# State products of a chunked scan as three split-operand matmuls, with the inputs' lower parts on GpSimd

## The chip, the cores and the metric

The kernel runs on one core of a Trainium2 chip. Its engines work side by side, each through its own queue of instructions in a fixed order, and wait for one another by semaphores: TensorE (PE in the profile; its weight loads are PEld), VectorE (DVE), ScalarE (ACT), GpSimd (POOL) and SyncE (SP), which issues most transfers. The metric is the device time of one execution in microseconds (us). Shorter is better.

## The reference

The program is one inference step of a small trunk: one Mamba-2 (SSD) layer, one pooling layer and a final norm, for a prompt of 1024 tokens and for 8 sampled sequences of 8 tokens each. The change lies in the SSD layer's scan. Cut to what it touches:

```python
T = min(CHUNK, L)            # 128 tokens
acum = jnp.cumsum(dt * A.reshape(G, R), axis=2)
CB = jnp.einsum('bctgn,bcsgn->bctsg', C, B)
xdt = x * dt[..., None]
y_intra = jnp.einsum('bctsgr,bcsgrp->bctgrp', CB[..., None] * decay, xdt)
decay_end = jnp.exp(acum[:, :, -1:] - acum)
chunk_states = jnp.einsum('bctgn,bctgr,bctgrp->bcgrpn', B, decay_end, xdt)
chunk_decay = jnp.exp(acum[:, :, -1])
def step(h, inp):
    s, d = inp
    return d[..., None, None] * h + s, h
h_final, h_prev = lax.scan(step, h0, (chunk_states, chunk_decay))
y_inter = jnp.einsum('bctgn,bctgr,bcgrpn->bctgrp', C, jnp.exp(acum), h_prev)
```

There are 32 heads of 64 channels in 8 groups of 4; a group shares B and C, with a state of 128 numbers per channel. So for each group and each of the prompt's 8 chunks a chunk state is one product of B (128 tokens by 128 states, transposed) with the decayed inputs (128 tokens by 256 channels).

## The kernel before

`ssd_layer` runs eight calls of `scan_group`, one per group. Each is woven with other work by `weave`, which takes steps of two generators in turn: groups 0 to 6 with `proj_group`, the input projection and convolution of the next group, group 7 with the first units of the output projection. Beneath this a scheduler of the tile framework places every engine's instructions in an order of its own, by its planned costs, and puts in the waits; so a step of the code doesn't stay where the source has it.

Within a group, `front(c)` prepares chunk c and `back(c)` finishes it; the loop calls `front(c + 1)` ahead of `back(c)`. Chunk 8 is the sample chunk. The names are:

- `front`: `pt` (tag tr, two buffers in PSUM) holds CB and the transposes of the two x tiles and of B. M is the decay times CB: four Relus and an Exp on ScalarE (L526, L527), cb and the product on VectorE (L529, L530). `xd` (L532, VectorE, two buffers) holds the inputs twice, scaled by dt and by dt times the decay to the chunk's end. `Bt` (L536, ScalarE) is B's transpose, copied out of PSUM; in the sample chunk it is split into `Bt` and its lower part `Bl` (L539, L540). `ea` (L513, L545) is C times the decay from the chunk's start, and `cd` (L544) the chunk's decay.
- `back`: four heads' y products, M by xd and ea by h (L560, L564), two at a time on halves of TensorE's columns (column-tiled); their evacuation on VectorE (L550); the state product `S` (L567); `hd`, the old state times `cd`, on GpSimd (L573); and the new state `h`, hd plus S, on VectorE (L574; a plain copy, L570, in chunk 0).
- `back_sample` and `state_sample`: the sample's states, with masked copies of the split inputs (`st`, L612 and L613; `xm` and `xs`, L616 to L618) against `Bt` and `Bl` (L625, L626).
- `proj_group`: matmuls of 364 or 360 columns in three parts (`mm3`, L178 to L180: upper weights by upper activations, upper by lower, lower by upper), their evacuation (L386, L388), the convolution `conv_tile` (ScalarE L342, three taps on VectorE L344, tanh L347, L348, L350), and the split of the next weights into an upper part (ScalarE L135) and a lower part (VectorE L136). The gate's squares are summed on TensorE (`ms`, L664).

In this trace a matmul of float32 operands shows as two passes (two records) and one of operands of the type F32R as one. The kernel splits a float32 operand into a copy in F32R (the upper part) and the difference, in F32R as well (the lower part), and multiplies two such operands in three products: upper by upper, upper by lower, lower by upper.

Of the kernel before, what the change touches and what calls it, by code (L numbers as in the profile page):

```python
# [7 lines left out]
F32 = mybir.dt.float32  # L8
F32R = mybir.dt.float32r
AF = mybir.ActivationFunctionType  # L10
ALU = mybir.AluOpType
# [3 lines left out]
P = 128  # L15
# [78 lines left out]
class Build:  # L94
# [379 lines left out]
    def scan_group(self, g, T):  # L474
        nc, tk, gp, pp = self.nc, self.tk, self.gs, self.pp
        B, C, xs, zs = T[0], T[1], T[2:4], []
# [17 lines left out]
        def load_ac(c):  # L494
            if c < 8:
                j, cc = c // 2, c % 2
                t = gp.tile([P, 4, 128], F32, tag="acb", bufs=2, name=self.name("acb"))
                nc.sync.dma_start(t, self.acd[32 * j + 4 * g:32 * j + 4 * g + 4, 128 * cc:128 * cc + 128].unsqueeze(0).to_broadcast([P, 4, 128]))
            else:
                t = gp.tile([P, 4, 128], F32, tag="acb", bufs=2, name=self.name("acb"))[:, :, :64]  # L500
                nc.sync.dma_start(t, self.acd[96 + 4 * g:100 + 4 * g, 256:320].unsqueeze(0).to_broadcast([P, 4, 64]))
            acbs[c] = t

        def front(c):

            j, cc, L = (c // 2, c % 2, 128) if c < 8 else (0, 2, 64)
            col = 32 * j + 4 * g
            t0 = 128 * c
            tok = slice(t0, t0 + L)
            acb = acbs.pop(c)  # L510
            load_ac(c + 1) if c < 8 else None
            ea = gp.tile([P, 4, 128], F32, tag="ea", bufs=2, name=self.name("ea"))
            nc.scalar.activation(ea[:, :, :L], acb, AF.Exp)  # L513
            pt = pp.tile([P, 512], F32, tag="tr", bufs=2, name=self.name("tr"))
            nc.tensor.matmul(pt[:L, 384:384 + L], B[:, tok], C[:, tok], start=True, stop=True)
            for i, t in enumerate((xs[0], xs[1], B)):
                o = pt[:, 128 * i:128 * i + 128]
                if c < 8:
                    nc.tensor.transpose(o, t[:, tok], self.ident)
                else:  # L520
                    self.dup(o, t[:, tok])

            M = gp.tile([P, 4, 128], F32, tag="M", bufs=2, name=self.name("M"))
            mask = self.kc[:L, K_MASK:K_MASK + 128] if c < 8 else self.kc[:64, K_SMASK:K_SMASK + 64]
            for r in range(4):
                nc.scalar.activation(M[:L, r, :L], acb[:L, r, :], AF.Relu, bias=tk["ac", cc][:L, col + r:col + r + 1], scale=-1.0)  # L526
            nc.scalar.activation(M[:L, :, :L], M[:L, :, :L], AF.Exp, scale=-1.0)  # L527
            cb = gp.tile([P, 128], F32, tag="cb", bufs=1, name=self.name("cb"))
            nc.vector.tensor_tensor(out=cb[:L, :L], in0=pt[:L, 384:384 + L], in1=mask, op=ALU.mult)  # L529
            nc.vector.tensor_tensor(out=M[:L, :, :L], in0=M[:L, :, :L], in1=cb[:L, :L].unsqueeze(1).to_broadcast([L, 4, L]), op=ALU.mult)  # L530
            xd = gp.tile([P, 2, 4, 64], F32, tag="xd", bufs=2, name=self.name("xd"))
            nc.vector.tensor_tensor(out=xd, in0=pt[:, 0:256].rearrange("p (r q) -> p r q", r=4).unsqueeze(1).to_broadcast([P, 2, 4, 64]),  # L532
                                    in1=tk["x", cc][:, :, col:col + 4].unsqueeze(3).to_broadcast([P, 2, 4, 64]), op=ALU.mult)
            if c < 8:
                Bt = gp.tile([P, 128], F32, tag="Bt", bufs=2, name=self.name("Bt"))
                nc.scalar.activation(Bt, pt[:, 256:384], AF.Copy)  # L536
            else:
                Bt = tuple(gp.tile([P, 128], F32R, tag=s, bufs=2, name=self.name(s)) for s in ("Bt", "Bl"))
                nc.scalar.activation(Bt[0], pt[:, 256:384], AF.Copy)  # L539
                nc.vector.tensor_tensor(out=Bt[1], in0=pt[:, 256:384], in1=Bt[0].bitcast(F32), op=ALU.subtract)  # L540
            cd = None
            if 0 < c < 8:
                cd = gp.tile([P, 4], F32, tag="cd", bufs=2, name=self.name("cd"))
                nc.scalar.activation(cd, acb[:, :, 127], AF.Exp)  # L544
                nc.vector.tensor_tensor(out=ea, in0=C[:, tok].unsqueeze(1).to_broadcast([P, 4, 128]), in1=ea, op=ALU.mult)  # L545
            return tok, M, xd[:, 0], xd[:, 1], Bt, cd, ea

        def evac_y(py, q, tok, L):
            y = xs[q]
            nc.vector.scalar_tensor_tensor(out=y[:, tok], in0=y[:, tok], scalar=self.vec[:, V_D + 2 * g + q:V_D + 2 * g + q + 1], in1=py[:, :L],  # L550
                                           op0=ALU.mult, op1=ALU.add)

        def back(c, F):
            nonlocal h
            tok, M, xdt, xde, Bt, cd, ct = F
            for q in range(2):
                py = pp.tile([P, 512], F32, tag="y", bufs=2, name=self.name("y"))
                for rr in range(2):
                    r, o = 2 * q + rr, slice(64 * rr, 64 * rr + 64)
                    nc.tensor.matmul(py[o, :128], xdt[:, r, :], M[:, r, :], start=True, stop=(h is None))  # L560
                if h is not None:
                    for rr in range(2):
                        r, o = 2 * q + rr, slice(64 * rr, 64 * rr + 64)
                        nc.tensor.matmul(py[o, :128], h[:, r, :], ct[:, r, :], start=False, stop=True)  # L564
                evac_y(py, q, tok, 128)
            S = pp.tile([P, 512], F32, tag="S", bufs=1, name=self.name("S"))
            nc.tensor.matmul(S[:, :256], Bt, xde.rearrange("p r q -> p (r q)"), start=True, stop=True)  # L567
            hn = gp.tile([P, 4, 64], F32, tag="h", bufs=3, name=self.name("h"))
            if h is None:
                nc.vector.tensor_copy(hn.rearrange("p r q -> p (r q)"), S[:, :256])  # L570
            else:
                hd = gp.tile([P, 4, 64], F32, tag="hd", bufs=1, name=self.name("hd"))
                nc.gpsimd.tensor_tensor(out=hd, in0=h, in1=cd.unsqueeze(2).to_broadcast([P, 4, 64]), op=ALU.mult)  # L573
                nc.vector.tensor_tensor(out=hn, in0=hd, in1=S[:, :256].rearrange("p (r q) -> p r q", r=4), op=ALU.add)  # L574
            h = hn
# [19 lines left out]
        def back_sample(F, zsc):  # L595
            tok, M, xdt, xde, Bt, _, ea = F
            for q in range(2):
                py = pp.tile([P, 512], F32, tag="y", bufs=2, name=self.name("y"))
                for rr in range(2):
                    r, o = 2 * q + rr, slice(64 * rr, 64 * rr + 64)  # L600
                    nc.tensor.matmul(py[o, :64], xdt[:64, r, :], M[:64, r, :64], start=True, stop=False)
                for rr in range(2):
                    r, o = 2 * q + rr, slice(64 * rr, 64 * rr + 64)
                    nc.tensor.matmul(py[o, :64], zsc[:, r, :], self.kc[:, K_SEL64:K_SEL64 + 64], start=False, stop=True)
                evac_y(py, q, tok, 64)
            for i in range(2):
                nc.gpsimd.tensor_tensor(out=h0[i], in0=h0[i],
                                        in1=ea[:, :, 32 * i + 7:32 * i + 32:8].rearrange("p r b -> p b r").unsqueeze(3).to_broadcast([P, 4, 4, 64]), op=ALU.mult)

            xv = xde.rearrange("p r q -> p (r q)")  # L610
            st = gp.tile([P, 256], F32R, tag="xl", bufs=1, name=self.name("st"))
            nc.scalar.activation(st, xv, AF.Copy)  # L612
            nc.vector.tensor_tensor(out=st[64:], in0=xv[64:], in1=st[64:].bitcast(F32), op=ALU.subtract)  # L613
            xms = []
            for b2 in range(4):
                xm = gp.tile([P, 2, 256], F32R, tag=("xm", "xs")[b2 % 2], bufs=2, name=self.name("xs"))  # L616
                for i in range(2):
                    nc.scalar.activation(xm[:, i], st.bitcast(F32), AF.Copy, scale=self.kc[:, K_SEQ + 2 * b2 + i:K_SEQ + 2 * b2 + i + 1])  # L618
                xms.append(xm.rearrange("p b n -> p (b n)"))
            return xms, Bt  # L620
# [10 lines left out]

        load_ac(0)
        F = front(0)
        yield
        for c in range(8):
# [1133 lines left out]
```

## Time and profile before

| | |
|---|---|
| time, median of 3 runs | 1660.68 us (1660.06 to 1662.37) |
| the profiled execution | 1660.51 us, of which the span is 1658.7 us |
| granted TensorE clock, mean | 0.994 |
| busy, share of the span | PE 98%, PEld 93%, DVE 79%, ACT 50%, POOL 29% |
| the scan | from about 265 to 880 us |
| DMA | 251 MB in all, mean 151 GB/s |

The profile gives one execution. Its page has the busy time of each engine over the span, the same in 40 equal slices with the clock that TensorE was granted, the chain of work that ended last, and the costliest groups of instructions by source line. Views of the trace give single instructions in a stretch of time (start and duration in us, then engine, line, operation, output and inputs, shape and count; in brackets the idle time before it and what ended it), the waits of an engine by what they were for, and sums by stretch. The durations of matmuls overlap, since they are pipelined: what a matmul costs is the distance between the ends of two of them.

### The profile page before, as it was taken

The page shows a single profiled execution, that of the slowest core. Times are in us where ns is not written, and L with a number is a line of the kernel's source. Part 1 is how long each engine was busy: PE and PEld are TensorE (multiplying, and loading weights), DVE is VectorE, ACT ScalarE, POOL GpSimd, SP SyncE. Part 2 cuts the span into 40 slices and gives each one's busy share as a digit, 9 for nine tenths or more (in the row PEclk, how much of TensorE's full clock was granted, in tenths as well). Part 3 has the DMA queues.
Part 4 walks back from the last instruction along what each step waited for, and adds up shares of the span by engine and source line. Part 5 has one row for each costly group of instructions (what it writes and reads, how often), then busy time and mean ns, then how long its engine had stood idle before and what let it go on. Part 6 is the DMA issues. An engine that isn't in the chain of part 4 may idle for free.

```text
span 1658.7 us, 30808 instructions
## 1 busy us (share of the span) xinstructions
PE 1627.5 (98%) x11965; PEld 1535.6 (93%) x11965; DVE 1310.9 (79%) x2240; ACT 821.6 (50%) x1606; POOL 474.4 (29%) x504
## 2 busy tenths in 40 slices
PE   8999999999999999999899999999999999999997
PEld 6899999888898988888789999999999999999997
DVE  6897687787777787788887556999999978577886
ACT  6644335767666676767552125633333234233364
POOL 0124441313132222313010012366666640000241
PEclk9999999999999999999999999999999999999999
DMA  8423226455453534353877123123323359655773
GB/s 341 160 81 121 79 69 216 121 160 163 135 177 108 172 119 144 108 177 116 291 242 266 50 75 129 38 98 131 108 96 112 125 175 362 210 148 173 170 171 119
DMA packets 115971, 251.07 MB, mean 151 GB/s; under 512 B 17489, under 2 KB 58609, under 8 KB 115825
## 3 DMA queue, kind: packets, MB, share of 16 engines
q1 hardware_dynamic: 111792, 236.39, 42.0%
q0 software_dynamic: 4032, 12.72, 4.4%
q8 instruction: 94, 1.54, 0.4%
q14 instruction: 53, 0.43, 0.1%
HBM read 188.87 MB, written 57.98 MB: 149 GB/s over the span
## 4 chain that ended last, share of the span: by engine, by line
PE 35%; POOL 8%; issue 7%; DVE 5%; ACT 1%; DMA 1%; SPq 0%; DVEq 0%; POOLq 0%; ACTq 0%
PE mm L178 6%; PE mm L179 6%; PE mm L180 6%; PE op L1149 2%; PE op L1150 2%; PE op L1148 2%; POOL w L172 2%; PE st L934 2%; PE st L933 1%; PE st L932 1%; POOL sw L898 1%; POOL sw L897 1%; POOL npl L787 1%; POOL wr L902 1%; POOL npl L788 1%
## 5 line engine op out<-in xcount | busy, mean ns | idle before, releaser
L178 PE MATMUL mm<-hh,wh 128*128 128x364 f32 x720 | 248.4, 345 | 0.0
L179 PE MATMUL mm<-hl,wh 128*128 128x364 f32 x720 | 239.0, 332 | 0.0
L180 PE MATMUL mm<-hh,wl 128*128 128x364 f32 x720 | 237.6, 330 | 0.0
L934 PE MATMUL st<-hh,w 128*128 128x272 f32 x704 | 203.2, 289 | 0.5 <-DVE w L172 0.5
L933 PE MATMUL st<-hl,w 128*128 128x272 f32 x704 | 203.1, 289 | 0.0
L932 PE MATMUL st<-hh,w 128*128 128x272 f32 x704 | 202.9, 288 | 0.0
L934 PE MATMUL st<-t,w 128*128 128x272 f32 x528 | 152.4, 289 | 4.3 <-POOL w L172 3.5
L933 PE MATMUL st<-t,w 128*128 128x272 f32 x528 | 152.2, 288 | 0.7 <-DVE t L1339 0.7
L932 PE MATMUL st<-t,w 128*128 128x272 f32 x528 | 151.7, 287 | 0.0
L573 POOL TENSOR_TENSOR hd<-h,cd 128x256 f32<-128x256 f32 x56 | 67.1, 1199 | 282.3 <-DVE h L574 142.4
L344 DVE SCALAR_TENSOR_TENSOR raw<-raw,cwh,raw 128x1112 f32<-128x1112 f32 x96 | 134.3, 1399 | 9.4 <-ACT raw L342 8.7
L178 PEld LDWEIGHTS mm<-hh,wh 128*128 128x128 f32 x720 | 135.4, 188 | 5.5 <-ACT raw L386 1.6
L179 PEld LDWEIGHTS mm<-hl,wh 128*128 128x128 f32 x720 | 135.5, 188 | 4.6 <-issue 3.0
L180 PEld LDWEIGHTS mm<-hh,wl 128*128 128x128 f32 x720 | 135.3, 188 | 3.0 <-issue 2.9
L932 PEld LDWEIGHTS st<-hh,w 128*128 128x128 f32 x704 | 132.8, 189 | 0.3 <-issue 0.3
L934 PEld LDWEIGHTS st<-hh,w 128*128 128x128 f32 x704 | 132.4, 188 | 0.7 <-DVE w L172 0.7
L933 PEld LDWEIGHTS st<-hl,w 128*128 128x128 f32 x704 | 132.5, 188 | 0.0
L1149 PE MATMUL op<-b,w 128*128 128x272 f32 x448 | 129.0, 288 | 1.1 <-DVE b L1078 1.1
L178 PE MATMUL mm<-gh,wh 128*128 128x364 f32 (+1 forms) x384 | 128.6, 337 | 1.2 <-ACT gh L693 1.2
L1148 PE MATMUL op<-b,w 128*128 128x272 f32 x448 | 129.5, 289 | 0.0
L1150 PE MATMUL op<-b,w 128*128 128x272 f32 x448 | 129.1, 288 | 0.1
L179 PE MATMUL mm<-gl,wh 128*128 128x364 f32 (+1 forms) x384 | 126.9, 331 | 2.2 <-DVE gl L694 2.2
(292 smaller groups left out, 4563.0 us busy)
## 6 DMA issues: line engine op xcount, KB each, us to landing
wr<-win SPq DMA_DIRECT2D x48, 512.0 KB, 4.7
acb<-acd SPq DMA_DIRECT2D x64, 256.0 KB, 3.6
wr<-pin SPq DMA_DIRECT2D x32, 512.0 KB, 3.6
wr<-pout SPq DMA_DIRECT2D x28, 512.0 KB, 4.0
wr<-pout POOLq DMA_DIRECT2D x20, 512.0 KB, 5.8
x<-xT SPq DMA_DIRECT2D x16, 544.0 KB, 6.9
zsd<-z SPq DMA_DIRECT2D x16, 544.0 KB, 2.7
z<-zsd SPq DMA_DIRECT2D x16, 544.0 KB, 5.8
```

Source lines behind the costliest of these rows:

```text
L172: eng.tensor_tensor(out=lo, in0=src, in1=hi.bitcast(F32), op=ALU.subtract)
L178: nc.tensor.matmul(ps[:, :n], hi[:, k, :], ah[:, a:a + n], start=first, stop=False)
L179: nc.tensor.matmul(ps[:, :n], hi[:, k, :], al[:, a:a + n], start=False, stop=False)
L180: nc.tensor.matmul(ps[:, :n], lo[:, k, :], ah[:, a:a + n], start=False, stop=last)
L344: nc.vector.scalar_tensor_tensor(out=acc[:, :n], in0=raw[:, k:k + n], scalar=w[k], in1=acc[:, :n], op0=ALU.mult, op1=ALU.add)
L573: nc.gpsimd.tensor_tensor(out=hd, in0=h, in1=cd.unsqueeze(2).to_broadcast([P, 4, 64]), op=ALU.mult)
L932: nc.tensor.matmul(ps[c][:, :QUART], hi[:, k], xh[:, t], start=(k == 0), stop=False)
L933: nc.tensor.matmul(ps[c][:, :QUART], hi[:, k], xl[:, t], start=False, stop=False)
L934: nc.tensor.matmul(ps[c][:, :QUART], lo[:, k], xh[:, t], start=False, stop=(k == 3))
L1148: nc.tensor.matmul(ps[:, :QUART], hi[:, k], xh, start=k == 0, stop=False)
L1149: nc.tensor.matmul(ps[:, :QUART], hi[:, k], xl, start=False, stop=False)
L1150: nc.tensor.matmul(ps[:, :QUART], lo[:, k], xh, start=False, stop=k == 7)
```

## The change

In all chunks `Bt` is now split into an upper and a lower F32R part, as the sample chunk's was; so `Bl`, a subtraction on VectorE, is new in 64 chunks. The decayed inputs are split as well: ScalarE copies them into the F32R tile `xm[0]`, and GpSimd subtracts that from the original into `xm[1]`, both in `front`. The state product becomes three accumulating F32R matmuls of 256 columns: upper by upper, upper B by lower inputs, lower B by upper inputs. The sample's masked copies take their tags in another order (two of `xm` and then two of `xs`, where they alternated), since the chunks' `xm` tiles now share that tag's two buffers.

In the order that the scheduler makes of it TensorE's queue is the same ahead of the first state product and behind the last of group 7. The three products of one chunk often don't stand together: in chunk 0 of groups 1 to 6 the first is ahead of the y products and the other two behind them, and in chunk 2 matmuls of the projection lie between. In chunk 3 of these groups all three stand ahead of the chunk's y products, which stood ahead of S before. On GpSimd chunk 3's subtraction stands behind that chunk's `hd`. SyncE's order has the same length as before.

```diff
@@ in front(c)
+            Bt = tuple(gp.tile([P, 128], F32R, tag=s, bufs=2, name=self.name(s)) for s in ("Bt", "Bl"))
+            nc.scalar.activation(Bt[0], pt[:, 256:384], AF.Copy)
+            nc.vector.tensor_tensor(out=Bt[1], in0=pt[:, 256:384], in1=Bt[0].bitcast(F32), op=ALU.subtract)
+            xe = xd[:, 1]
             if c < 8:
-                Bt = gp.tile([P, 128], F32, tag="Bt", bufs=2, name=self.name("Bt"))
-                nc.scalar.activation(Bt, pt[:, 256:384], AF.Copy)
-            else:
-                Bt = tuple(gp.tile([P, 128], F32R, tag=s, bufs=2, name=self.name(s)) for s in ("Bt", "Bl"))
-                nc.scalar.activation(Bt[0], pt[:, 256:384], AF.Copy)
-                nc.vector.tensor_tensor(out=Bt[1], in0=pt[:, 256:384], in1=Bt[0].bitcast(F32), op=ALU.subtract)
+
+                xv = xe.rearrange("p r q -> p (r q)")
+                xt = gp.tile([P, 2, 256], F32R, tag="xm", bufs=2, name=self.name("xm"))
+                xe = xt[:, 0], xt[:, 1]
+                nc.scalar.activation(xe[0], xv, AF.Copy)
+                nc.gpsimd.tensor_tensor(out=xe[1], in0=xv, in1=xe[0].bitcast(F32), op=ALU.subtract)
...
-            return tok, M, xd[:, 0], xd[:, 1], Bt, cd, ea
+            return tok, M, xd[:, 0], xe, Bt, cd, ea
@@ in back(c, F)
             S = pp.tile([P, 512], F32, tag="S", bufs=1, name=self.name("S"))
-            nc.tensor.matmul(S[:, :256], Bt, xde.rearrange("p r q -> p (r q)"), start=True, stop=True)
+            for i, (a, b) in enumerate(((0, 0), (0, 1), (1, 0))):
+                nc.tensor.matmul(S[:, :256], Bt[a], xde[b], start=(i == 0), stop=(i == 2))
@@ in back_sample(F, zsc)
-                xm = gp.tile([P, 2, 256], F32R, tag=("xm", "xs")[b2 % 2], bufs=2, name=self.name("xs"))
+                xm = gp.tile([P, 2, 256], F32R, tag=("xm", "xs")[b2 // 2], bufs=2, name=self.name("xs"))
```

## The prediction

> **What bounds the kernel now.** I read the page's first part, then the table of windows over the scan, then the waits, then single lines and stretches of the timeline.
>
> ```profile
> PE 1627.5 (98%) x11965; PEld 1535.6 (93%) x11965; DVE 1310.9 (79%) x2240; ACT 821.6 (50%) x1606; POOL 474.4 (29%) x504
> 340.00:580.00 240.00, 240.00 (x1792) 214.43 (x1791) 184.81 (x308) 159.87 (x353) 58.71 (x85) 1.00 0.48 148
> 265.00:880.00 615.00, 607.76 (x4539) 536.37 (x4538) 486.04 (x831) 407.64 (x908) 141.63 (x197) 0.99 0.52 166
> PE y L560 <- DVE M L530: 1.3, 2, 0.8
> ```
>
> The first row is the whole span (busy us, share, instructions). The next two are stretches, with the busy time of PE, PEld, DVE, ACT and POOL, then the granted clock, the DMA share and GB/s. In 340 to 580 PE is busy in all 240.00 us at clock 1.00; in the whole scan, 265 to 880, in 607.76 of 615. The last row is the largest wait of a scan matmul on M: 1.3 us in two stalls. So TensorE bounds the scan, the others follow with slack, and only two things can move the time: TensorE's own work, and new stalls on it.
>
> **The change, part by part: TensorE's work.** The state product S is one F32 matmul that runs as two passes:
>
> ```profile
> L567 PE MATMUL S<-xd,Bt x128: 377/379/483, 273.4 to 856.5; 128*128 128x256 f32 x128
> 609.70 0.28 PE L564 MATMUL y<-ea,h 128*64 128x128 f32 x2
> 609.91 0.48 PE L567 MATMUL S<-xd,Bt 128*128 128x256 f32 x1
> 610.23 0.38 PE L567 MATMUL S<-xd,Bt 128*128 128x256 f32 x1
> ```
>
> A row gives start, duration, engine, line. Matmuls are pipelined, so the price of one is the distance between ends. The passes end at 610.39 and 610.61: 0.22 us each (0.216 by the pace of such passes elsewhere in the scan), 0.432 for the product. The 128 passes are 64 products. The y products before them, on half the columns of the array, end at 609.98; the first pass needs 0.41, so the step from column-tiled to full-array work costs 0.41 - 0.216 = 0.19.
>
> The three F32R products of 256 columns have no row here; the nearest are F32R matmuls of 272 and 360 columns:
>
> ```profile
> 1099.93 0.29 PE L933 MATMUL st<-t,w 128*128 128x272 f32 x1
> 1102.93 0.29 PE L933 MATMUL st<-hl,w 128*128 128x272 f32 x1
> 604.13 0.33 PE L180 MATMUL mm<-hh,wl 128*128 128x360 f32 x1
> 607.63 0.33 PE L180 MATMUL mm<-hh,wl 128*128 128x360 f32 x1
> ```
>
> From 1099.93 to 1102.93 lie 24 intervals: 3.00/24 = 0.125 us. From 604.13 to 607.63 lie 21: 0.167. Both are 0.46 ns a column, so 256 columns take 0.118 and three products 0.353. Saved: 0.432 - 0.353 = 0.079 per product, 64 x 0.079 = 5.1 us. The bounds: three at the 272-column price are 0.375 (3.6 us saved); if these products ran no faster than an F32 pass, 0.65 and 14 us lost.
>
> The Trainium skill ("TensorE: Matmul & The Clock Gate", section "Wait — 56ns, not 53.3ns?") states a start-to-start time of columns over 2.4 GHz plus about 2.5 ns. That estimates 0.109 for 256 columns, so 0.328 for three and 1.6 us more saved; but it gives 0.116 for 272 columns where this trace has 0.125, and the trace decides.
>
> Against the saving stands the order. The build places the three products apart: in chunk 0 the first goes ahead of the y products and the others after them. The scan's PE order has 118 column-tiled stretches before and 125 after. A stretch costs the 0.19 above at its end and this at its start:
>
> ```profile
> 580.20 0.38 PE L567 MATMUL S<-xd,Bt 128*128 128x256 f32 x1
> 580.51 0.33 PE L560 MATMUL y<-M,xd 128*64 128x128 f32 x2
> 580.67 0.50 PE L560 MATMUL y<-M,xd 128*64 128x128 f32 x6
> ```
>
> The first pair of y records ends 0.26 after the S pass (580.58 to 580.84), the next three end at 581.17, 0.11 each: 0.15 for the step. Seven stretches more: 7 x 0.34 = 2.4 us. TensorE's own work thus shrinks by 5.1 - 2.4 = 2.7 us.
>
> **Work added elsewhere.** Each of 64 chunks gains a copy on ScalarE, a subtraction on VectorE (Bl) and one on GpSimd:
>
> ```profile
> L612 ACT ACTIVATE st<-xd x8: 405/406/408, 322.2 to 856.6; 128x256 fp32r<-128x256 f32 x8
> L540 DVE TENSOR_TENSOR Bl<-tr,Bt x8: 274/278/292, 322.4 to 856.8; 128x128 fp32r<-128x128 f32 x8
> L573 POOL TENSOR_TENSOR hd<-h,cd x56: 613/930/2819, 281.5 to 849.8; 128x256 f32<-128x256 f32 x56
> ```
>
> (ns, least/median/most.) The like work of the sample chunk and of hd prices them: 64 x 0.406 = 26 us on ScalarE, 64 x 0.278 = 18 on VectorE, 64 x 0.61 to 0.93 = 39 to 60 on GpSimd. All three engines have room in the window row above (407.64, 486.04 and 141.63 of 615), so the sums cost nothing; what counts is lateness. SP's order has the same length, and no DMA is added. The new F32R tiles change no transfer. The transpose tile tr is now released after Bl as well, the buffers of xd after ScalarE's copy and GpSimd's subtraction; both are wanted again two chunks on, some 10 us, far longer than any delay below. The sample's new tags only fix which buffer the next group's first tiles inherit: those of its first half, read first. I take nothing for it.
>
> **Where S can be late.** The second product needs GpSimd's result. hd shows what delays that engine:
>
> ```profile
> 587.03 0.61 POOL L573 TENSOR_TENSOR hd<-h,cd 128x256 f32<-128x256 f32 x1 [3.74 <-DVE h L574]
> 594.04 2.82 POOL L573 TENSOR_TENSOR hd<-h,cd 128x256 f32<-128x256 f32 x1 [4.52 <-DVE h L574]
> 593.88 1.37 DVE L344 SCALAR_TENSOR_TENSOR raw<-raw,cwh,raw 128x1112 f32<-128x1112 f32 x1
> 595.16 1.22 DVE L136 TENSOR_TENSOR wl<-wr,wh 128x1024 fp32r<-128x1024 f32 x1
> 596.30 0.28 DVE L529 TENSOR_TENSOR cb<-tr,kc 128x128 f32<-128x128 f32 x1
> 686.56 1.68 POOL L573 TENSOR_TENSOR hd<-h,cd 128x256 f32<-128x256 f32 x1 [2.20 <-DVE h L574]
> 686.40 1.37 DVE L344 SCALAR_TENSOR_TENSOR raw<-raw,cwh,raw 128x1112 f32<-128x1112 f32 x1
> 687.69 1.64 DVE L136 TENSOR_TENSOR wl<-wr,wh 128x1024 fp32r<-128x1024 f32 x1
> ```
>
> With VectorE idle, hd takes 0.61. Begun at 594.04 inside a tap of the convolution (L344, both inputs in SBUF), it ends at 596.86: 0.48 after L136, the second such operation, has ended at 596.38. At 686.56 it ends at 688.24, 0.47 after the first (687.77), and there L136 is held to 1.64 instead of 1.22. So a GpSimd subtraction that begins inside such an operation waits for one or two of them.
>
> The Trainium skill ("SBUF — State Buffer", section "SBUF: two separate sides") states that VectorE with two SBUF inputs and GpSimd hold a shared port pair as an exclusive lock, each for its whole instruction. By that the wait is one operation, as at 686.56; the trace has two at 594.04.
>
> Now the chunks of a group, walked through in group 4 (groups 1 to 6 have nearly the same order). In chunk 0 S is bound by its inputs already:
>
> ```profile
> 578.78 0.68 DVE L532 TENSOR_TENSOR xd<-tr,tkx 128x512 f32<-128x512 f32 x1
> 579.55 0.28 ACT L536 ACTIVATE Bt<-tr 128x128 f32<-128x128 f32 x1 [1.42 <-DVE xd L532]
> 579.92 0.66 PE L567 MATMUL S<-xd,Bt 128*128 128x256 f32 x2
> ```
>
> S starts 0.09 after Bt ends (579.83). The copy behind Bt ends near 580.15, when the order puts the first product at about 580.2: no stall. GpSimd then meets no two-input operation of VectorE for 0.9 us and is done near 580.8; the second product, now behind four y products, comes at 581.1. Chunks 1, 2 and 4 to 7 leave the subtraction 0.35 to 2 us before its product in the order of the changed build. In chunk 3 it is tight:
>
> ```profile
> 584.21 0.66 PE L664 MATMUL ms<-z,ones 128*32 128x272 f32 x6
> 589.01 1.31 ACT L342 ACTIVATE raw<-raw,cwh 128x1112 f32<-128x1112 f32 x1
> 590.80 0.26 ACT L536 ACTIVATE Bt<-tr 128x128 f32<-128x128 f32 x1
> 590.96 0.63 ACT L527 ACTIVATE M<-M 128x512 f32<-128x512 f32 x1
> ```
>
> Counted on from the ms products (end 584.87) through the new PE order at the paces above, S(3)'s first product is due at 594.3 and the second at 594.4, since they now stand ahead of the y products. ScalarE ends L527 at 591.59; ahead of it the new order puts the copy of chunk 2 (0.23 late), L513 (0.5) and one L526 more (0.3), and behind it comes the copy of chunk 3: done near 592.95. VectorE starts the first L344 when L342 is done (590.32 plus 0.23 and 0.5, so 591.05), then Bl, then the second L344 from 592.55 to 593.9. The subtraction, behind hd on GpSimd, thus begins inside it. After one operation it is done at 593.9 + 0.48 = 594.4: no stall. After two (M, 0.6) at 595.0, and if hd has held the first L344 for 0.4 as at 686.56, at 595.4: a stall of 1.0. Between 0 and 1.0 no row decides, one operation and two both occur; I take the middle, 0.5, in six groups: 3.0 us. While TensorE waits there, its queue behind S waits (the projection's matmuls, then y(3)), and that is the cost. M of chunk 3, 1.05 late on ScalarE by the same three items, is multiplied on VectorE between 594.5 and 595.4, and y(3) is due at 595.3 without the stall: it lies in the shadow of S. Chunk 3's ea and the next evacuations behind ScalarE's copy come 0.4 later, and nothing reads them within 2 us. Group 0, whose two M stalls above can grow or go, adds 1 us to each side of the range.
>
> **The sum.** -2.7 + 3.0 = +0.3 on the profiled execution's 1660.51 gives 1660.8. That execution is 0.17 below the median 1660.68, so 1661.0 against the median. No difference can be told from noise within 0.2%, 3.3 us.
>
> **The rivals.** (1) No stall in chunk 3, because GpSimd gets in after one operation, as at 686.56: -2.7, so 1658.0, still within 0.2%. (2) Faster: no stall, and the seven added stretches cost less than the two steps I read off one place each. Free, they leave the whole 5.1; at a third of the 2.4 us it is -5.1 + 0.8 = -4.3, so 1656.4. It decides where the steps cost under 1.8 us together. For it: a step's price is part of a pipelined row, and the new stretches lie between products that differ from those rows; against it: both steps were read at places where TensorE waited for nothing. The clock-gate page of the Trainium skill, quoted above, gives a time near this one by another way. (3) Slower: in chunk 3 the subtraction passes only behind three operations, L344, M and the third L344 (595.8), and is done at 596.3: 1.9 us late, six times 11.4, +8.7, so 1669.4. It decides from 1.0 per group, (2.7 + 3.3)/6. For it: VectorE is packed there without a gap (ScalarE's M is ready by then), and hd's 2.82; against it: no row shows a wait behind three. That rule of the port lock, which the Trainium skill also gives ("GPSIMD Engine Reference", section "1. Specifications": interfaces shared with VectorE when it has two SBUF inputs), speaks against the change; the trace agrees, with 0.61 against 2.82. (4) The products don't run faster: 3 x 0.216 is 14 us more, 1677; only the missing 256-column row speaks for it.
>
> **How the numbers follow.** Forecast (a stall of 0.2 to 1.0 in chunk 3) 0.37; (1) 0.13; (2) 0.13; (3) 0.34, with a price between 3.3 and 12; (4) 0.03. Faster is (2), 0.13; same the forecast and (1), 0.50; slower (3) and (4), 0.37. The range runs from (2)'s 1656.4 to 1668.5, which leaves out the far end of (3) and (4); the forecast alone has 1659.2 to 1664.2.
>
> **What would show it.** S: three records whose ends lie 0.118 apart. 125 column-tiled stretches. Waits of S on GpSimd's xm in chunk 3 of groups 1 to 6, none elsewhere in the scan; GpSimd's subtractions at 0.61 in chunk 0 and over 1 in chunk 3. TensorE's sum in the scan lower by about 2.7. Wrong would be: stalls of y or of the transposes on VectorE, whose Bl and held operations I price at nothing; stalls of S in chunks other than 3; products slower than 0.125.

## The result and the profile after

The changed kernel takes 1663.63 us (median of 20 runs, 1660.55 to 1666.41); the kernel before, run beside it, 1660.03. The ratio is 1.0020 (95% interval 1.0014 to 1.0026), so it is slower by 2.3 to 4.3 us. The profiled execution took 1663.08 us, with a span of 1661.3.

The same rows as shown of before, from the page's first part, the windows and TensorE's waits in the scan (us in total, times, longest):

```profile
PE 1630.6 (98%) x12029; PEld 1536.0 (92%) x12029; DVE 1341.7 (81%) x2304; ACT 841.0 (51%) x1670; POOL 523.7 (32%) x568
340.00:580.00 240.00, 239.04 (x1800) 212.37 (x1799) 194.87 (x327) 167.09 (x376) 75.21 (x109) 1.00 0.46 149
265.00:880.00 615.00, 607.49 (x4579) 534.37 (x4581) 513.26 (x891) 424.54 (x969) 189.22 (x260) 0.99 0.50 163
PE S L572 <- POOL xm L544: 1.6, 6, 0.3
PE S L630 <- DVE h L633: 1.3, 1, 1.3
PE y L564 <- DVE M L530: 0.3, 1, 0.3
```

In 340 to 580 TensorE was busy in all 240.00 us before; now 0.96 is idle. S waits for GpSimd in six places, and a product of the sample's states waits 1.3 us for VectorE. But the waits understate the loss: the rows of consecutive matmuls overlap, so only the part of a wait that outlasts the matmul ahead shows as idle (0.28 us of 0.55 in the case below). I therefore measure a stall as the distance between the ends of two matmuls less what the pair costs elsewhere.

Chunk 3 of group 5, from the timeline of the changed kernel:

```profile
670.93 0.36 PE L572 MATMUL S<-xm,Bt 128*128 128x256 f32 x1
671.58 0.39 PE L572 MATMUL S<-xm,Bt 128*128 128x256 f32 x1 [0.28 <-POOL xm L544]
671.80 0.28 PE L572 MATMUL S<-xm,Bl 128*128 128x256 f32 x1
669.31 0.42 ACT L543 ACTIVATE xm<-xd 128x256 fp32r<-128x256 f32 x1
667.61 1.83 DVE L344 SCALAR_TENSOR_TENSOR raw<-raw,cwh,raw 128x1112 f32<-128x1112 f32 x1
669.57 1.36 DVE L344 SCALAR_TENSOR_TENSOR raw<-raw,cwh,raw 128x1112 f32<-128x1112 f32 x1
670.86 1.21 DVE L530 TENSOR_TENSOR M<-M,cb 128x512 f32<-128x512 f32 x1
667.65 0.62 POOL L578 TENSOR_TENSOR hd<-h,cd 128x256 f32<-128x256 f32 x1 [0.95 <-DVE h L579]
669.80 1.72 POOL L544 TENSOR_TENSOR xm<-xd,xm 128x256 fp32r<-128x256 f32 x1 [1.53 <-ACT xm L543]
```

The first product ends at 671.29, the second at 671.97, the third at 672.08. The third is 0.11 behind the second (0.118 in the median of the scan); the second is 0.66 behind the first, a stall of 0.55 (from unrounded ends). The chain begins on GpSimd: hd, started 0.04 after the first tap (L344), is through in 0.62 and holds that tap to 1.83 instead of 1.37; the second tap starts at 669.57; the copy is done at 669.73, and GpSimd's subtraction begins at 669.80, inside that tap. It ends at 671.52, 0.59 after the tap (670.93), and M behind it (L530) is held to 1.21 instead of 0.68.

The stall is 0.55 in five groups and 0.24 in group 4: 3.0 us in all. In group 4 hd and the first tap went the other way round:

```profile
593.17 1.38 DVE L344 SCALAR_TENSOR_TENSOR raw<-raw,cwh,raw 128x1112 f32<-128x1112 f32 x1
593.22 1.80 POOL L578 TENSOR_TENSOR hd<-h,cd 128x256 f32<-128x256 f32 x1 [0.95 <-DVE h L579]
```

Here hd is held (1.80 for 0.62) and the tap is not, so the second tap is over earlier and the subtraction, begun at the same point, gets through in 1.42: 0.30 less, as the stall is.

Two kinds of stall that I did not have, first S in chunk 0 and then the transposes of chunk 5:

```profile
656.27 0.32 PE L178 MATMUL mm<-hh,wh 128*128 128x360 f32 x1
656.53 0.38 PE L572 MATMUL S<-xm,Bt 128*128 128x256 f32 x1
655.89 0.28 ACT L535 ACTIVATE Bt<-tr 128x128 fp32r<-128x128 f32 x1 [1.83 <-DVE xd L532]
656.07 0.41 ACT L543 ACTIVATE xm<-xd 128x256 fp32r<-128x256 f32 x1
603.90 0.33 PE L180 MATMUL mm<-hh,wl 128*128 128x360 f32 x1
604.26 0.35 PE L515 MATMUL tr<-xbc,xbc 128*128 128x128 f32 x1
603.16 0.76 DVE L350 SCALAR_TENSOR_TENSOR xbc<-raw,raw 128x64 f32<-128x64 f32 x1
603.84 0.28 DVE L536 TENSOR_TENSOR Bl<-tr,Bt 128x128 fp32r<-128x128 f32 x1
```

In chunk 0 S ends 0.32 after the projection's matmul (656.59 to 656.91), 0.20 more than 0.118: it starts 0.05 after ScalarE's copy ends (656.48), and 0.05 to 0.06 after it in all six groups. They make 1.2 us. The transposes end 0.38 behind the matmul ahead of them (0.109 elsewhere), a stall of 0.28 in groups 1 to 4, 1.1 us: they start 0.147 after chunk 4's Bl has ended (604.12), which still reads the buffer that they fill, and 0.147 in the other three groups too. L350 ahead of it took 0.76, 0.22 elsewhere, with a GpSimd subtraction beside it. The third:

```profile
786.53 0.32 PE L180 MATMUL mm<-hh,wl 128*128 128x364 f32 x1
788.14 0.50 PE L630 MATMUL S<-xs,Bt 128*128 128x512 f32 x1 [1.29 <-DVE h L633]
777.48 2.13 DVE L549 TENSOR_TENSOR ea<-xbc,ea 128x512 f32<-128x512 f32 x1
779.92 2.65 DVE L661 TENSOR_TENSOR xbc<-xbc,z 128x1088 f32<-128x1088 f32 x1
777.13 4.29 POOL L612 TENSOR_TENSOR h<-h,ea 128x1024 f32<-128x1024 f32 x2 [5.43 <-PE Z L593]
```

The sample's last products wait 1.56 us in group 6. VectorE is late there because ea (0.68 elsewhere) and the gate's product (L661, 1.50 before) stand beside GpSimd's 1024-wide products of the sample states; in the kernel before ea began 1.2 us ahead of those. This is read from the rows; no run tests it by itself.

The balance over the scan, in us. TensorE's own work is what is left of its time when all stalls are taken off:

| | before | after | difference |
|---|---|---|---|
| TensorE's own work, from 264 us to the last ms product | 595.9 | 593.0 | -2.9 |
| column-tiled stretches in it | 117.5 | 124.5 | +7 |
| stalls: S in the chunks | 0 | 4.7 | +4.7 |
| stalls: transposes behind Bl | 0 | 1.1 | +1.1 |
| stalls: products for the sample | 0 | 1.9 | +1.9 |
| stalls: y (on M and evacuations) | 2.6 | 0.5 | -2.1 |
| all other stalls | 14.4 | 15.3 | +0.9 |
| end of the scan | 876.87 | 880.51 | +3.6 |

The 4.7 us of S are 3.0 in chunk 3, 1.2 in chunk 0 and 0.5 once in group 0. The 1.9 of the sample are the 1.56 above and a wait of 0.37 in group 0.

Two limits of this table. How the +3.6 divides between own work and other stalls hangs on which distance counts as a pair's cost: other choices give -1.5 to -3.1 for the first row. And each side is a single execution: the run below that changes only tags has the very TensorE order of the kernel before, and its scan ends at 878.37, 1.5 us later. The stalls that recur in four to six groups are firm, the single ones less so.

After the scan the two profiled executions come 1 us closer again, with no instruction changed there; that is left to the spread of the runs.

### The profile page after: what moved, and what is told of

Same layout as the page of the kernel before. It is cut to its first block, busy times and chain, and to the rows that moved or that the text cites. A ratio compares the mean times of both kernels' runs of the same rounds, so it can differ in the third digit from the quotient of the medians.

```text
span 1661.3 us, 31193 instructions
## 1 busy us (share of the span) xinstructions
PE 1630.6 (98%) x12029; PEld 1536.0 (92%) x12029; DVE 1341.7 (81%) x2304; ACT 841.0 (51%) x1670; POOL 523.7 (32%) x568
## 3 DMA queue, kind: packets, MB, share of 16 engines
q8 instruction: 95, 1.56, 0.4%
## 4 chain that ended last, share of the span: by engine, by line
PE 33%; POOL 8%; issue 7%; DVE 6%; ACT 1%; DMA 1%; SPq 0%; DVEq 0%; POOLq 0%; ACTq 0%
PE mm L178 6%; PE mm L179 6%; PE mm L180 6%; PE op L1154 2%; PE op L1155 2%; PE op L1153 2%; POOL w L172 2%; PE st L939 2%; PE st L938 1%; PE st L937 1%; POOL sw L902 1%; POOL sw L903 1%; POOL npl L792 1%; POOL wr L907 1%; POOL npl L793 1%
## 5 line engine op out<-in xcount | busy, mean ns | idle before, releaser
L178 PE MATMUL mm<-hh,wh 128*128 128x364 f32 x720 | 241.4, 335 | 0.0
L344 DVE SCALAR_TENSOR_TENSOR raw<-raw,cwh,raw 128x1112 f32<-128x1112 f32 x96 | 138.0, 1437 | 9.1 <-ACT raw L342 8.2
L544 POOL TENSOR_TENSOR xm<-xd,xm 128x256 fp32r<-128x256 f32 x64 | 64.7, 1012 | 214.4 <-ACT xm L543 133.1
```

Of the source, the lines that this page charges most:

```text
L178: nc.tensor.matmul(ps[:, :n], hi[:, k, :], ah[:, a:a + n], start=first, stop=False)
L344: nc.vector.scalar_tensor_tensor(out=acc[:, :n], in0=raw[:, k:k + n], scalar=w[k], in1=acc[:, :n], op0=ALU.mult, op1=ALU.add)
L544: nc.gpsimd.tensor_tensor(out=xe[1], in0=xv, in1=xe[0].bitcast(F32), op=ALU.subtract)
```

## The experiments

Theory: the products save what they should, and the loss is TensorE waiting for the lower parts. Rival: the added work on the other engines, and the order that the scheduler makes of it, are the loss, whoever waits for what.

**The lower inputs computed, but not read.**

```diff
-            for i, (a, b) in enumerate(((0, 0), (0, 1), (1, 0))):
+            for i, (a, b) in enumerate(((0, 0), (0, 0), (1, 0))):
```

> The second product reads the inputs' upper part again instead of their lower part (so the lower part of the inputs is left out of S), and GpSimd still computes the lower part, which nothing reads. TensorE's order stays that of the changed kernel. Theory (the loss is TensorE waiting for GpSimd): the stalls of S in chunk 3 go, 5 of 0.55 us and one of 0.24, 3.0 us in all; those of chunk 0 (0.2 each, 1.2 in all, on ScalarE's copy) and of the transposes behind Bl (1.1) stay. Time 3 us below the changed kernel, within 1.5 us of the kernel before. Rival (the added work on the other engines and the new order are the loss, whatever S waits for): as the changed kernel, 3 to 4 us above before.

Measured: 1661.42 us, ratio to before 1.0009 (1.0000 to 1.0018), 2 us below the changed kernel; the scan ends 2.3 us earlier. Chunk 3 of group 5 again (timeline):

```profile
668.75 1.72 POOL L544 TENSOR_TENSOR xm<-xd,xm 128x256 fp32r<-128x256 f32 x1 [1.53 <-ACT xm L543]
669.84 0.48 PE L572 MATMUL S<-xm,Bt 128*128 128x256 f32 x2
670.16 0.28 PE L572 MATMUL S<-xm,Bl 128*128 128x256 f32 x1
```

GpSimd takes the same 1.72 us, and the three products run through (the pair ends at 670.32, the third at 670.44). So the stall of chunk 3 is the wait for GpSimd. It isn't saved whole: y, 0.2 late on M, stood in the shadow of S, as the prediction said, and now stalls there in four of the six groups (in the other two hd was held and the first tap was not, as in group 4 above). The stalls of chunk 0 and of the transposes stay, and the sample's too.

**All the side work, S as before.**

```diff
-            for i, (a, b) in enumerate(((0, 0), (0, 1), (1, 0))):
-                nc.tensor.matmul(S[:, :256], Bt[a], xde[b], start=(i == 0), stop=(i == 2))
+            nc.tensor.matmul(S[:, :256], Bt[0].bitcast(F32), xde[2], start=True, stop=True)
```

(`xde[2]` is the unsplit input.)

> All the splitting is done as in the changed kernel, but S is one F32 matmul of the rounded transpose of B (its lower part is left out) with the whole inputs, so TensorE's work is that of before and S waits for no lower part. Theory: what is left of the loss is what the added work does by itself, that is the transposes behind Bl (1.1 us) and VectorE being late once in group 6 (1.6), less the stalls of y that went (2.1): 0 to +2 us against before. Rival (the added work is the loss): the changed kernel's 3.6 plus the 2.9 us that its three products save, about +6.5 us.

Measured: 1665.47 us against 1660.49, ratio 1.0039 (1.0025 to 1.0052): nearer to the rival. The transposes stall by 1.2 us and the sample by 0.9, as in the changed kernel; by ends the y products take 2.6 us more than before (the order now breaks y pairs apart in chunk 7, and its first pair ends 0.24 behind the transposes instead of beside them). The rest I have not followed; the order differs too, so it may lie there. This is the run that the theory missed: the side work, with the order that it brings, costs 5 us without any product waiting for a lower part.

**The lower inputs last.**

```diff
-            for i, (a, b) in enumerate(((0, 0), (0, 1), (1, 0))):
+            for i, (a, b) in enumerate(((0, 0), (1, 0), (0, 1))):
```

> The product with the inputs' lower part comes third instead of second. Theory: in chunk 3 one product of 0.118 us lies between, so the stall shrinks from 0.55 to 0.43, six times, 0.7 us in all; chunk 0 is unchanged. Time 0.5 to 1 us below the changed kernel, which is hard to tell in the time and is to be read in the stalls of the trace. Rival (the stall is of the first product, or of Bl): the stall of chunk 3 stays at 0.55 or moves to the product with Bl.

Measured: 1663.18 us, ratio 1.0018 (1.0009 to 1.0027), 0.45 below the changed kernel, less than the runs can tell. The trace has it:

```profile
670.93 0.36 PE L572 MATMUL S<-xm,Bt 128*128 128x256 f32 x1
671.13 0.28 PE L572 MATMUL S<-xm,Bl 128*128 128x256 f32 x1
671.63 0.39 PE L572 MATMUL S<-xm,Bt 128*128 128x256 f32 x1 [0.21 <-POOL xm L544]
```

The product with Bl follows at once; the one with GpSimd's part ends 0.60 after it (from unrounded ends) instead of 0.66 after the first. The stall is 0.48, not 0.43, because GpSimd began 0.06 later; and it is 0.48 in group 4 too, which had 0.24: there hd now takes 0.61 and holds the first tap, as in the other groups. So the six make 2.9 us, for 3.0: the last place is worth what was said in a group and nothing in the sum.

**The subtraction on VectorE.**

```diff
-                nc.gpsimd.tensor_tensor(out=xe[1], in0=xv, in1=xe[0].bitcast(F32), op=ALU.subtract)
+                nc.vector.tensor_tensor(out=xe[1], in0=xv, in1=xe[0].bitcast(F32), op=ALU.subtract)
```

> The lower part of the inputs is subtracted on VectorE instead of GpSimd. The scheduler then makes 43 more column-tiled stretches on TensorE than in the changed kernel (166 against 123 by its order). At 0.347 us a stretch that is 15 us, and VectorE gets 64 subtractions of about 0.4 us, 26 us more of 615 with 513 busy. Theory (a stretch costs 0.347 us wherever it stands): 15 us above the changed kernel, less up to 3 us of its stalls of S, so 12 to 15 above it. Rival (the steps are partly hidden, so stretches cost less): under 8 us above it.

Measured: 1682.49 us, ratio 1.0137 (1.0124 to 1.0151), 19 above the changed kernel. It lies above what either foresaw. The trace has 173.5 stretches, 49 more than the changed kernel, and TensorE's own work is 12.4 us longer: 0.25 a stretch, not 0.347. The rest is lateness, above all in the first output units beside group 7 (TensorE's waits):

```profile
PE mm L178 <- ACT gh L698: 7.5, 2, 6.5
PE S L630 <- DVE xbc L554: 3.3, 3, 1.3
```

So one line of the code that names another engine moves the time by 19 us, about 12 of them, by this count, through TensorE's order.

**The chunk's y products held together, S behind them.** The first y product gets added waits on M, ea, h and the inputs' lower part (the lines that add them):

```diff
+                    if r == 0:
+                        for i in w + ([hi] if hi is not None else []):
+                            self.tc.add_manual_dep(ym.ins, i.ins.name, mybir.DependencyInfo(mybir.DependencyClass.Sync, mybir.DependencyReason.DATA), reason="block")
```

(`w` holds the instructions of M and ea and the GpSimd subtraction; `hi` is that of h.)

> The changed kernel with one thing added: the first y product of a chunk waits for M, ea, the old state and the inputs' lower part, so the chunk's y products stand together and S behind them. By the order of the build the scan has 109 column-tiled stretches for the changed kernel's 123. Theory (stretches cost 0.347 us each, and S in chunk 3 is late by 0.55 because it stands ahead of y): 14 x 0.347 = 4.9 us less, and of the 3.0 us of stalls in chunk 3 nothing left, since y and some projection matmuls now come first: 5 to 8 us below the changed kernel, 1 to 4 below the kernel before. Rival (y now waits for what it did not need, and the stall moves to y): less than 2 us below the changed kernel, with waits of y on GpSimd or VectorE in the trace.

Measured: 1657.91 us against 1660.81, ratio 0.9986 (0.9977 to 0.9995): 5.7 below the changed kernel and 2.9 below before. Chunk 3 of group 4 (timeline):

```profile
593.49 1.49 POOL L544 TENSOR_TENSOR xm<-xd,xm 128x256 fp32r<-128x256 f32 x1 [0.51 <-ACT xm L543]
598.85 0.39 PE L571 MATMUL y<-ea,h 128*64 128x128 f32 x4
599.17 0.51 PE L575 MATMUL S<-xm,Bt 128*128 128x256 f32 x2
599.51 0.28 PE L575 MATMUL S<-xm,Bl 128*128 128x256 f32 x1
```

GpSimd is held as before (1.49), but done at 594.98, 4 us ahead of S. 116.5 stretches are left, 8 fewer, and TensorE's own work is 3.4 us shorter, 0.43 a stretch (with the same room for other counts as in the balance; 1.4 is the least that I get).

**S behind y in chunk 0 as well.**

```diff
+                if i == 0:
+                    self.tc.add_manual_dep(mm.ins, ym.ins.name, mybir.DependencyInfo(mybir.DependencyClass.NoSync, mybir.DependencyReason.DATA), reason="s_after_y")
```

> As the one before, and the first product of S comes after the chunk's last y product too, in chunks 0 and 2 as well. The count of stretches stays at 109. Theory: the stall of S in chunk 0 (0.2, six times) goes as well, 1.2 us below the one before. Rival: the wait goes to whatever comes first in chunk 0, and the time is the same.

Measured: 1660.03 us, ratio 0.9996 (0.9987 to 1.0005): 2 us above the one before, not 1.2 below. The rival held and more: with S behind y, y waits in chunk 0 for the subtraction instead.

```profile
PE y L564 <- POOL xm L544: 2.5, 6, 0.5
```

**The same holding in the kernel before.** The edit of the run before last, with M, ea and h, and S still the one F32 product.

> The kernel before with its y products held together in the same way, S still one F32 product: 107 stretches by the order, 117 before. Theory: 10 x 0.347 = 3.5 us less than before. It tells whether what the reordered split kernel gains is the split's or the order's: the split's own saving of 5.0 us would make the split kernel 1 to 4 us faster than this one, if its stalls are gone; the rival (the split's side work eats its saving in any order) makes them equal or this one faster.

Measured: 1656.24 us, ratio 0.9971 (0.9961 to 0.9980): 4.6 us less than before, the fastest of all. 9 stretches fewer, TensorE's own work 4.1 us shorter (0.46 each; 2.7 is the least by other counts). The split kernel with the same holding is 1.7 us slower in the medians; their intervals overlap by 0.0003. In the profiled executions the two scans end together (874.23 and 874.28). So the split is no faster in a better order either, where S waits for GpSimd in chunk 3 no more: the point goes to the rival. But the orders are not the same: the split kernel keeps 8 more stretches (116.5 for 108.5), some 2.7 us at the 0.34 of the prediction, and 1.7 us of stalls of S, mostly in chunk 0. In one and the same order the two have not been compared.

**The tags alone, in the kernel before.**

```diff
-                xm = gp.tile([P, 2, 256], F32R, tag=("xm", "xs")[b2 % 2], bufs=2, name=self.name("xs"))
+                xm = gp.tile([P, 2, 256], F32R, tag=("xm", "xs")[b2 // 2], bufs=2, name=self.name("xs"))
```

> The kernel before with only the tags of the sample's masked copies changed. Theory (nothing, as the prediction has it; the stall at the last sample product of group 6 comes of VectorE's later work): within 0.1% of before and no stall of 1.3 us or more of the sample's products. Rival (the tags make the sample's copies wait): that stall appears here.

Measured: ratio 0.9997 (0.9988 to 1.0006), and no stall of the sample's products in group 6. The tags alone are not the cause.

**Bl not read from the transposes' tile.**

```diff
-            nc.vector.tensor_tensor(out=Bt[1], in0=pt[:, 256:384], in1=Bt[0].bitcast(F32), op=ALU.subtract)
+            if c < 8:
+                nc.vector.tensor_tensor(out=Bt[1], in0=Bt[0].bitcast(F32), in1=Bt[0].bitcast(F32), op=ALU.subtract)
+            else:
+                nc.vector.tensor_tensor(out=Bt[1], in0=pt[:, 256:384], in1=Bt[0].bitcast(F32), op=ALU.subtract)
```

> In the prompt's chunks Bl is the upper part less itself (zero, so the lower part of B is left out of S): a VectorE subtraction that no longer reads the transposes' PSUM tile. Theory (the transposes of chunk 5 wait 0.28 us in groups 1 to 4 because Bl, late on VectorE, still reads their buffer): those waits go, 1.1 us, and with 119 stretches by the order for 123 another 1.4, so 2 to 3 us below the changed kernel; chunk 3's stall of S stays. Rival (the wait is for something else that reads the tile, cb or xd): the 0.28 us stay.

Measured: 1663.07 us, ratio 1.0016 (1.0007 to 1.0025), 0.6 below the changed kernel, not 2 to 3. The stalls of 0.28 on the transposes are gone from all groups. By itself that doesn't settle it, because the new order also puts these transposes behind the modulation's products, where the kernel before had them. What does is the distance: in the changed kernel and the first three runs the transposes of chunk 5 stall 16 times, by 0.27 to 0.30, and start 0.145 to 0.147 after the end of Bl each time, while the other readers of the buffer, cb, xd and Bt, ended 2.1 us earlier or more. So Bl is the cause. The time did not follow: the new order lets subtractions of other chunks come late (TensorE's waits),

```profile
PE S L575 <- POOL xm L547: 1.8, 3, 0.8
```

and S stalls 0.23 in chunk 2 of six groups and 1.1 in two later chunks, 3.5 us where the changed kernel had 3.0 in chunk 3.

**The products alone.**

```diff
-            nc.vector.tensor_tensor(out=Bt[1], in0=pt[:, 256:384], in1=Bt[0].bitcast(F32), op=ALU.subtract)
+            if c == 8:
+                nc.vector.tensor_tensor(out=Bt[1], in0=pt[:, 256:384], in1=Bt[0].bitcast(F32), op=ALU.subtract)
...
-                nc.gpsimd.tensor_tensor(out=xe[1], in0=xv, in1=xe[0].bitcast(F32), op=ALU.subtract)
...
-            for i, (a, b) in enumerate(((0, 0), (0, 1), (1, 0))):
+            for i, (a, b) in enumerate(((0, 0), (0, 0), (0, 0))):
```

(In the sample chunk Bl stays.)

> S is three F32R products of the upper parts alone; neither Bl nor the inputs' lower part is computed in the prompt's chunks (so both are left out of S), only ScalarE's copies remain. It shows what the products save by themselves. The order has 128 stretches, 123 in the changed kernel, so 1.7 us more for that. Theory (of the changed kernel's 6.4 us of added stalls, GpSimd and VectorE make 3.0 + 1.1 + 1.6): 5.7 - 1.7 = 4 us below the changed kernel, about the time of before. Rival (the loss is ScalarE's copies and the order alone): no faster than the changed kernel.

Measured: 1657.22 us against 1660.54, ratio 0.9978 (0.9970 to 0.9987): 3.3 below before and 6.4 below the changed kernel, more than the 4 expected, with 12 stretches more than before. There is no stall of S or of the transposes of 0.1 or more, though ScalarE's copies are there. So three products do save, and the two subtractions, one on GpSimd and one on VectorE, with the order that they bring, cost 6.4 us: more than the gain. What the order has of this and what the lateness, this run does not separate.

## Why the prediction was right or wrong

The time lies in the stated range. Whether it is within 0.2% of before is not clear: the ratio's interval goes on both sides of 1.002. Forecast was +0.3 us; measured were +3.6 in the medians and +2.6 between the two profiled executions.

- **TensorE's own work: right.** -2.7 forecast, -2.9 measured (-1.5 to -3.1 by other counts). A product takes 0.118 us, as the 272- and 360-column rows gave it. The 0.109 estimated from the Trainium skill's page "TensorE: Matmul & The Clock Gate", section "Wait — 56ns, not 53.3ns?", is not borne out by these rows. Seven stretches more were seven, though their price is less fixed than I took it: 5.0 - 2.9 leaves 0.30 each here, and other orders gave 0.25 to 0.46 around my 0.34.
- **Chunk 3: right in mechanism, and in size by luck.** Forecast 0.5 us in six groups, 3.0; measured 0.55 in five and 0.24 in one, 3.0. The 0.5 was the middle of two cases, one operation with no stall and two with 1.0, and neither came: GpSimd passes behind one operation, but hd has held the first tap by 0.46 before, which I had counted only with the two. That the wait is for GpSimd is shown by the run that does not read the lower inputs. The Trainium skill's "SBUF — State Buffer", section "SBUF: two separate sides", with its exclusive lock for a whole instruction, agrees with these rows (one operation waited for, 0.59 after its end), not with the two of hd before.
- **Chunk 0: wrong.** The step "The copy behind Bt ends near 580.15, when the order puts the first product at about 580.2: no stall" failed. S stalled 0.20 on ScalarE's copy, six times, 1.2 us. The copy was priced right, but the product's place was earlier than I counted, and a margin of 0.05 us is none.
- **Buffers: wrong.** "both are wanted again two chunks on, some 10 us, far longer than any delay below" does not hold for the transposes' tile. The modulation's products (`am`, L253) take a tile of the same tag between chunks 4 and 5, so chunk 5 gets the buffer of chunk 4, one chunk on; and the order puts chunk 4's Bl behind the convolution's last steps, so it ends 0.147 us ahead of the transposes, which wait for it. That makes 1.1 us. It is shown by the constant distance in 16 stalls; the run with Bl off that tile took the stall away and not the time.
- **VectorE's work at nothing: wrong.** The forecast named stalls of y or the transposes on VectorE, and stalls of S outside chunk 3, as what would refute it. Both came: the transposes on Bl (1.1 us) and S in chunk 0 (1.2). One more came in the sample (1.6). Against them the two M stalls of group 0 shrank and those of evacuations in groups 5 and 6 went, -2.1 together; I had only the first two, as a bound of 1 us.
- **The rivals.** (3), three operations waited for in chunk 3, did not occur; the kernel was slower by another way, small stalls in four places. (1) and (2) did not occur. (4) is refuted by 0.118.

The likeliest case had the one stall that it named and the sign of the small difference. It missed 4.7 us of other new stalls (1.2 and 0.5 of S, 1.1 of the transposes, 1.9 of the sample), which I priced at zero after a walk through one group by hand, and the 2.1 us that y stalls less; that these partly cancel is luck as well. What stays open: how much of the side work's cost (5.0 us in the medians of the second run) is lateness and how much the order, since every edit changes both.

## What to carry to other kernels

Where TensorE is busy throughout, a saving on it can be paid back in stalls when its operands come from engines that hold one another up: price the added work at the margin of its tightest place in each period, not at the engine's room. 0.05 us of slack is no cover. And where a scheduler writes the order, count the steps between column-tiled and full work first: here holding a chunk's tiled products together gave 4.6 us, no less than the 3.3 that the three products gave by themselves (the two intervals overlap).

## What was not expected of the hardware

A matmul's wait shows as idle time only where it outlasts the matmul ahead: stalls of 0.55 us by ends appear as 0.28 in the list of waits, and those of 0.20 not at all. And the hold goes both ways: GpSimd's subtractions, 0.73 us alone, took up to 1.72 beside two-input work of VectorE, and held that in turn, M from 0.68 to 1.21 and the tail L350 from 0.22 to 0.76.

Which of two such operations passes first can hang on nanoseconds. In chunk 3 of groups 1 to 6, hd starts just after the first tap. In the changed kernel and four of the runs (the first three and the one with Bl off the transposes' tile) that makes 30 cases. The 19 that started 0.037 to 0.046 us after the tap were through in 0.61 to 0.62, and the tap took 1.82 to 1.83. The 11 that started 0.047 to 0.092 us after it took 1.76 to 1.80, and the tap 1.38. So the same pair costs TensorE 0.55 us in one group and 0.24 in the next, with no difference in the program.
